# A weight's low part written by ScalarE and finished by a GpSimd DMA instead of VectorE: one layer in split float32

## The chip, the cores and the metric

The kernel runs on one core of one Trainium2 chip. The metric is the device time of one execution in microseconds (us), shown as a median of several. Each profile below is of one execution, with the time of every instruction on the engines: PE is TensorE, DVE is VectorE, ACT is ScalarE, POOL is GpSimd, SP is SyncE, which here issues loads and stores.

## The reference: one encoder layer

One layer on 512 tokens of 1024 features, all in float32:

```
x = LN1(alpha*x + 0.5*SwiGLU1(x))                 # weights 1024x2816, 1024x2816, 2816x1024
h = x @ w_in                                      # q, k, v, indexer q/k/w, conv B, C, u
A = attention over the 128 keys that an indexer picks for each query (ALiBi, softmax)
B = bg * causal_conv3(cg * u)
x = LN2(alpha*x + concat(A, B) @ w_out)
x = LN3(alpha*x + 0.5*SwiGLU2(x))
x = x + sigmoid(x @ ple_gate_w) * (p @ ple_proj_w)
```

## The kernel before: every operand in two parts

**Two parts.** TensorE multiplies in a rounded format (float32r). So every operand is kept as a high part, `hi = round(w)`, and a low part, `lo = w - hi`, and a product is the sum of three matmuls: hi with hi, and twice a high part with a low part. The second of the three to four matmuls on a block already needs a low part, so a weight of which only the high part is there lets PE go on for one or two matmuls at most. `split` (line 110) makes the parts: ACT casts (line 111), DVE subtracts (line 112).

**Weights.** `unit` (line 114) brings in a piece of a weight of 128 x 1024 values (512 KB): a load issued by SP (line 118) into a raw page, then `split` into a high and a low page, then the raw page is free again. There are 98 such pieces in the program: all of the down projections (44), `w_in` (29, one of them narrower), `w_out` (8), `ple_gate_w` (8), `ple_proj_w` (2) and `p` (1), and the gate and up weights of three plain chunks (6): the second chunk of the first SwiGLU and the first two of the second. The gate and up weights of the other chunks go through `weights` (line 270), which forms sums of quarter blocks (seven products instead of eight) and splits these with `split` itself.

**Pages.** All weights, hidden chunks and projections live in 38 pages of 4 KB per partition, handed out first in, first out. A load waits until the last reader of its page is done, and SP issues its loads in order.

**Order.** A scheduler orders each engine's instructions by priorities; `unit` raises the priority of its load and its split by a number (`AHEAD...`) so that they run ahead of their use. On the chip each engine runs its own list strictly in order and waits at its head. POOL's list has few entries: index tables (lines 536 and 537) and, for each of the three layer norms, four tiny powers (line 160), whose results DVE needs for the last step of the norm (line 162), after which PE transposes the block (line 146).

**Places that the prediction names.** The start: two plain chunks of the first SwiGLU. The end of the first SwiGLU, where the last down-projection pieces come in (PE line 132). The end of the attention, where `w_out` is multiplied. The end of the second SwiGLU, and behind it the gate (`ple_gate_w`), whose eight pieces are read in order, three matmuls each.

Of the kernel before, what the change touches and what calls it, by code (L numbers as in the profile page):

```python
# [10 lines left out]
ALU = mybir.AluOpType  # L11
# [52 lines left out]
def layer_kernel(ctx: ExitStack, tc: tile.TileContext, x, ln1_g, ln1_b, ffn1_wg, ffn1_wu, ffn1_wd, w_in,  # L64
                 conv_w, w_out, ln2_g, ln2_b, ffn2_wg, ffn2_wu, ffn2_wd, ln3_g, ln3_b, ple_gate_w, ple_proj_w, x_t, p_t, out):
    nc = tc.nc
# [19 lines left out]
    def page(shape, dt=F32R):  # L86
        i = free_pages.pop(0)
        t = sb.tile(shape, dt, tag=f"pg{i}", name=f"pg{i}_{count('pg')}")
        owner[id(t)] = (i, t)
        return t  # L90

    def free(*tiles):
        for t in tiles:
            free_pages.append(owner.pop(id(t))[0])
# [15 lines left out]
    def split(hi, lo, src):  # L110
        nc.scalar.copy(hi, src)  # L111
        nc.vector.tensor_sub(lo, src, hi.bitcast(F32))  # L112

    def unit(src, shape, ahead=AHEAD):

        with tc.high_priority(offset=ahead):
            r = page(shape, F32)
            nc.sync.dma_start(r, src)
            hi, lo = page(shape), page(shape)
            split(hi, lo, r)  # L120
            free(r)
        return hi, lo

# [115 lines left out]
    def ffn(X, wg, wu, wd, ln_g, ln_b, first, load_nat, groups, nplain, ahead, ahead_f, ahead_d):  # L239
# [11 lines left out]
        def plain(fc, ws, cuts, ah):  # L251

            for nm, w in mats:
                if nm not in ws:
                    ws[nm] = unit(rows(w[:, fc * P:(fc + 1) * P], 0, NDC), [P, NDC, P], ah)
            ps = {nm: bank("all") for nm, _ in mats}
            for n in range(2):
                for nm, _ in mats:
                    mm(ps[nm][:, n * 256:(n + 1) * 256],
                       [((ws[nm][0][:, c], ws[nm][1][:, c]), tuple(z[:, c % 4] for z in X.q[f"B{c // 4 + 1}{n + 1}"])) for c in range(NDC)])  # L260
            for u in ws.values():
                free(*u)
            hf = ring("hf", 2, [P, 512])
            s_t = ring("a", 2, [P, 512])
            nc.scalar.activation(s_t, ps["g"], AF.Silu)
            nc.vector.tensor_mul(hf, s_t, ps["u"])
            return put(hf)
# [80 lines left out]
        for gi, per in enumerate(groups):  # L348
# [13 lines left out]
            def wd_rows(i, half):  # L362
                if (i, half) not in wds:
                    n2 = min(2, per - i)
                    u = unit(rows(wd[:, half * 512:(half + 1) * 512], (f0 + i) * P, n2), [P, n2, 512], ahead_d)
                    for k in range(n2):
                        wds[i + k, half] = (u[0][:, k], u[1][:, k])
                        held[i + k, half] = u if k == n2 - 1 else ()
                return wds[i, half]
# [38 lines left out]
    def embed_prep():  # L408
        p_T.extend(unit(rows(p_t, 0, 2), [P, 2, S], AHEAD_P))
        yield  # L410
        for k in range(2):
            wp.append(unit(rows(ple_proj_w[0], k * P, 1), [P, 1, 1024], AHEAD_P))
# [384 lines left out]
```

## Time and profile before

| | before |
|---|---|
| time, median of 3 | 1025.05 us (1024.97 to 1025.1) |
| the profiled execution's own time | 1026.09 us |
| its span, first to last instruction | 1024.0 us |
| PE busy | 1004.6 us (98%) |
| DVE busy | 822.2 us (80%) |
| ACT busy | 441.8 us (43%) |
| DMA from HBM | 101.49 MB |

The share of busy time is an average over stages. Times in a view count from the span's start; about 2 us of the execution lie outside the span. Where a group's row says `<-`, the name behind it is what ended the idle time, by its engine, its output and its line.

### The profile page before, as it was taken

The page shows a single profiled execution, that of the slowest core. Times are in us where ns is not written, and L with a number is a line of the kernel's source. Part 1 is how long each engine was busy: PE and PEld are TensorE (multiplying, and loading weights), DVE is VectorE, ACT ScalarE, POOL GpSimd, SP SyncE. Part 2 cuts the span into 40 slices and gives each one's busy share as a digit, 9 for nine tenths or more (in the row PEclk, how much of TensorE's full clock was granted, in tenths as well). Part 3 has the DMA queues.
Part 4 walks back from the last instruction along what each step waited for, and adds up shares of the span by engine and source line. Part 5 has one row for each costly group of instructions (what it writes and reads, how often), then busy time and mean ns, then how long its engine had stood idle before and what let it go on. Part 6 is the DMA issues. An engine that isn't in the chain of part 4 may idle for free.

```text
span 1024.0 us, 15507 instructions
## 1 busy us (share of the span) xinstructions
PE 1004.6 (98%) x6313; PEld 903.8 (88%) x6313; DVE 822.2 (80%) x1283; ACT 441.8 (43%) x621; POOL 25.0 (2%) x35
## 2 busy tenths in 40 slices
PE   8999999999999999999999999999999999999998
PEld 7989999898998878888878778989999898998787
DVE  7897868978697958999479988896868969689852
ACT  6444424433354235332576836443425324246221
POOL 1000000000000200000000011000000000000100
PEclk9999999999999999999999999999999999999999
DMA  9342324323335231424013223331424322227111
GB/s 311 122 123 83 109 98 131 97 83 107 100 119 185 69 92 42 128 58 124 20 42 104 83 65 101 124 124 39 127 83 144 103 79 87 83 85 265 52 41 51
DMA packets 99510, 104.57 MB, mean 102 GB/s; under 512 B 5872, under 2 KB 81904, under 8 KB 99440
## 3 DMA queue, kind: packets, MB, share of 16 engines
q1 hardware_dynamic: 99440, 103.60, 31.8%
q8 instruction: 49, 0.80, 0.3%
q14 instruction: 21, 0.17, 0.1%
HBM read 101.49 MB, written 2.10 MB: 101 GB/s over the span
## 4 chain that ended last, share of the span: by engine, by line
PE 89%; DMA 4%; DVE 3%; ACT 3%; issue 1%; POOLq 0%; SPq 0%; ACTq 0%
PE bk L132 86%; ACT pg L111 2%; DVE pg L112 1%; DMA pg<-in_ffn_wu_dram 1%; PE bk L506 1%; DMA pg<-in_w_in_dram 1%; DMA pg<-in_x_t_dram 1%; PE bk L507 1%; PE bk L704 1%; DMA pg<-in_ple_proj_w_dram 1%; DMA pg<-in_ffn_wd_dram 0%; PE bk L146 0%; ACT a L676 0%; DMA pg<-in_ple_gate_w_dram 0%; PE bk L692 0%
## 5 line engine op out<-in xcount | busy, mean ns | idle before, releaser
L132 PE MATMUL bk<-pg,pg 128*128 128x256 f32 (+1 forms) x2832 | 496.4, 333 | 4.4 <-ACT pg L111 1.8
L132 PEld LDWEIGHTS bk<-pg,pg 128*128 128x128 f32 x2832 | 427.6, 190 | 56.0 <-ACT pg L111 2.6
L111 ACT CAST pg<-pg 128x1024 fp32r<-128x1024 f32 (+1 forms) x267 | 260.0, 984 | 313.3 <-PE bk L132 78.4
L112 DVE TENSOR_TENSOR pg<-pg,pg 128x1024 fp32r<-128x1024 f32 (+1 forms) x267 | 300.6, 1139 | 40.6 <-ACT pg L111 35.5
L132 PE MATMUL bk<-xq,pg 128*128 128x256 f32 x2208 | 275.3, 284 | 4.6 <-DVE mv L158 1.5
L132 PEld LDWEIGHTS bk<-xq,pg 128*128 128x128 f32 x2208 | 270.6, 193 | 7.0 <-ACT pg L111 2.3
L132 PE MATMUL bk<-xT,pg 128*128 128x512 f32 (+2 forms) x600 | 133.0, 381 | 0.3 <-ACT xT L111 0.2
L132 PEld LDWEIGHTS bk<-xT,pg 128*128 128x128 f32 (+1 forms) x600 | 109.9, 186 | 21.5 <-ACT xT L111 0.5
L132 PE MATMUL bk<-pg,xT 128*128 128x512 f32 (+1 forms) x312 | 69.5, 374 | 1.3 <-DVE nat L385 1.3
L132 PEld LDWEIGHTS bk<-pg,xT 128*128 128x128 f32 x312 | 55.0, 188 | 11.4 <-ACT pg L111 1.8
L329 ACT ACTIVATE a<-pg 128x512 f32<-128x512 f32 x40 | 25.2, 629 | 71.7 <-DVE pg L338 66.1
L111 ACT CAST pg<-hf 128x512 fp32r<-128x512 f32 (+1 forms) x56 | 34.6, 618 | 35.2 <-DVE hf L330 19.6
L112 DVE TENSOR_TENSOR pg<-hf,pg 128x512 fp32r<-128x512 f32 (+1 forms) x56 | 38.3, 684 | 4.7 <-ACT pg L111 4.5
L399 DVE SCALAR_TENSOR_TENSOR nat<-bk,nat 128x512 f32<-128x512 f32 x64 | 40.4, 682 | 0.8 <-PE bk L132 0.7
L330 DVE TENSOR_TENSOR hf<-a,pg 128x512 f32<-128x512 f32 x40 | 27.5, 688 | 13.6 <-ACT a L329 13.5
L338 DVE TENSOR_TENSOR pg<-bk,pg 128x512 f32<-128x512 f32 x20 | 13.8, 692 | 29.9 <-PE bk L132 29.4
L160 POOL TENSOR_TENSOR mv<-mv,mhalf 128x1 f32<-128x1 f32 x12 | 17.8, 1480 | 627.0 <-DVE mv L159 627.0
L286 DVE TENSOR_TENSOR pg<-pg,pg 128x512 f32<-128x512 f32 x40 | 27.3, 686 | 5.7 <-DMA pg<-in_ffn_wg_dram 5.7
L292 DVE TENSOR_TENSOR pg<-pg 128x512 f32<-128x512 f32 x40 | 27.4, 686 | 2.9 <-PE bk L132 2.9
L112 DVE TENSOR_TENSOR pg<-bk,pg 128x512 fp32r<-128x512 f32 (+2 forms) x37 | 22.5, 626 | 8.5 <-ACT pg L111 8.1
L287 DVE TENSOR_TENSOR pg<-pg,pg 128x512 f32<-128x512 f32 x40 | 27.3, 685 | 0.0
L293 DVE TENSOR_TENSOR pg<-pg,pg 128x512 f32<-128x512 f32 x40 | 27.1, 686 | 0.1
(100 smaller groups left out, 612.7 us busy)
## 6 DMA issues: line engine op xcount, KB each, us to landing
pg<-in_ffn_wg_dram SPq DMA_DIRECT2D x44, 512.0 KB, 4.1
pg<-in_ffn_wu_dram SPq DMA_DIRECT2D x44, 512.0 KB, 4.7
pg<-in_ffn_wd_dram SPq DMA_DIRECT2D x44, 512.0 KB, 4.0
pg<-in_w_in_dram SPq DMA_DIRECT2D x28, 512.0 KB, 3.6
pg<-in_w_out_dram SPq DMA_DIRECT2D x8, 512.0 KB, 3.9
pg<-in_ple_gate_w_dram SPq DMA_DIRECT2D x8, 512.0 KB, 4.8
pg<-in_x_t_dram SPq DMA_DIRECT2D x4, 512.0 KB, 7.5
nat<-in_x_dram SPq DMA_DIRECT2D x4, 512.0 KB, 8.9
```

The source lines that it names most:

```text
L111: nc.scalar.copy(hi, src)
L112: nc.vector.tensor_sub(lo, src, hi.bitcast(F32))
L132: nc.tensor.matmul(ps, lhsT=st[a], rhs=mv[b], start=first and i == 0 and k == 0, stop=last and i == n - 1 and k == 2)
L160: nc.gpsimd.tensor_tensor(mv[:, 3:4], mv[:, 2:3], mhalf, op=ALU.pow)
L286: nc.vector.tensor_add(S1, A21, A22)
L287: nc.vector.tensor_sub(S2, S1, A11)
L292: nc.vector.tensor_sub(S3, A11, A21)
L293: nc.vector.tensor_sub(S4, A12, S2)
L329: nc.scalar.activation(s_t, e[m][:, :, 0], AF.Silu)
L330: nc.vector.tensor_mul(h3, s_t, e[m][:, :, 1])
L338: nc.vector.tensor_add(e[0][:, 1], prod("S4", "B22"), u4)
L399: nc.vector.scalar_tensor_tensor(dst, acc[t], CY, dst, op0=ALU.mult, op1=ALU.add)
```

## The change

In `unit` alone DVE's subtraction is gone. ACT writes the high part as before, and then a second time reads the raw page and writes its negative, rounded the same way, into the low page. Then a DMA issued by GpSimd adds the raw page to the low page where it lies: `-hi + w`. The raw page is free when this DMA has landed. `split` stays as it is everywhere else.

```diff
             r = page(shape, F32)
             nc.sync.dma_start(r, src)
             hi, lo = page(shape), page(shape)
-            split(hi, lo, r)
+            nc.scalar.copy(hi, r)
+
+            nc.scalar.mul(lo, r, -1.0)
+            nc.gpsimd.dma_start(lo, r, accum_op=ALU.add)
             free(r)
         return hi, lo
```

Lines behind this one move by three: a line 132 of before is a line 135 of the changed kernel, and a piece's own lines are 120 (cast), 122 (negative) and 123 (DMA).

The scheduler orders the engines anew. In the lists below `pg_n` is the n-th page handed out, the last number a running number. **POOL at the end of the program** held only the powers of the last norms:

```order
L160 TENSOR_TENSOR mv_5942<-mv_5942,mhalf 128x1
L160 TENSOR_TENSOR mv_5999<-mv_5999,mhalf 128x1
L160 TENSOR_TENSOR mv_9451<-mv_9451,mhalf 128x1
L160 TENSOR_TENSOR mv_9513<-mv_9513,mhalf 128x1
L160 TENSOR_TENSOR mv_9575<-mv_9575,mhalf 128x1
L160 TENSOR_TENSOR mv_9637<-mv_9637,mhalf 128x1
```

Now the DMAs of the gate's pieces stand among the last norm's four powers:

```order
L123 DMA pg_949_9771<-pg_947_9768 128x1024
L163 TENSOR_TENSOR mv_9541<-mv_9541,mhalf 128x1
L163 TENSOR_TENSOR mv_9603<-mv_9603,mhalf 128x1
L123 DMA pg_952_9778<-pg_950_9775 128x1024
L163 TENSOR_TENSOR mv_9665<-mv_9665,mhalf 128x1
L123 DMA pg_955_9785<-pg_953_9782 128x1024
L123 DMA pg_958_9792<-pg_956_9789 128x1024
L163 TENSOR_TENSOR mv_9727<-mv_9727,mhalf 128x1
L123 DMA pg_961_9799<-pg_959_9796 128x1024
```

The DMA of the gate's last piece (page 961) stands behind the last norm's fourth power.

**PE in the gate's first bank.** `ident,nat` are the transposes of the last norm's last block; the pieces' pages are 939 to 961 by threes, the first of a pair the high part. Before, 24 matmuls of the first bank and five of the second stood ahead of the transposes:

```order
L132 MATMUL bk_9705<-pg_957_9695,xT_3_9371 128x512
L132 MATMUL bk_9705<-pg_958_9696,xT_3_9371 128x512
L132 MATMUL bk_9705<-pg_957_9695,xT_3_9372 128x512
L132 MATMUL bk_9705<-pg_960_9701,xT_3_9371 128x512
L132 MATMUL bk_9705<-pg_961_9702,xT_3_9371 128x512
L132 MATMUL bk_9705<-pg_960_9701,xT_3_9372 128x512
L132 MATMUL bk_9736<-pg_939_9659,xT_3_9371 128x512
L132 MATMUL bk_9736<-pg_940_9660,xT_3_9371 128x512
L132 MATMUL bk_9736<-pg_939_9659,xT_3_9372 128x512
L132 MATMUL bk_9736<-pg_942_9665,xT_3_9371 128x512
L132 MATMUL bk_9736<-pg_943_9666,xT_3_9371 128x512
L146 MATMUL bk_9643<-ident,nat_71 128x128 x4
```

Now 20 of the first bank stand ahead of them, and four more behind them before the low page 961 is read:

```order
L135 MATMUL bk_9803<-pg_957_9791,xT_3_9455 128x512
L135 MATMUL bk_9803<-pg_958_9792,xT_3_9455 128x512
L149 MATMUL bk_9733<-ident,nat_71 128x128 x4
L149 MATMUL bk_9740<-ident,nat_71 128x128 x4
L135 MATMUL bk_9803<-pg_957_9791,xT_3_9456 128x512
L135 MATMUL bk_9803<-pg_960_9798,xT_3_9455 128x512
L135 MATMUL bk_9834<-pg_939_9749,xT_3_9455 128x512
L135 MATMUL bk_9834<-pg_940_9750,xT_3_9455 128x512
L135 MATMUL bk_9803<-pg_961_9799,xT_3_9455 128x512
```

So the transposes have come forward by nine matmuls.

**ACT at the end of the second SwiGLU** (920 to 950 us in the profile). Page 929 is the raw page of a down-projection piece, 930 its high and 931 its low page; line 329 is the activation of the last chunk. Before:

```order
L111 CAST pg_942_9665<-pg_941_9663 128x1024
L111 CAST pg_930_9415<-pg_929_9413 128x1024
L111 CAST pg_936_9439<-pg_935_9437 128x1024
L329 ACTIVATE a_9361<-pg_913_9167 128x512
L111 CAST pg_924_9388<-pg_923_9386 128x1024
L111 CAST pg_917_9364<-hf_9360 128x512
```

Now:

```order
L120 CAST pg_930_9502<-pg_929_9500 128x1024
L332 ACTIVATE a_9445<-pg_913_9251 128x512
L122 ACTIVATE pg_931_9503<-pg_929_9500 128x1024
L111 CAST pg_917_9448<-hf_9444 128x512
L120 CAST pg_924_9473<-pg_923_9471 128x1024
L122 ACTIVATE pg_925_9474<-pg_923_9471 128x1024
```

The negative of page 929 stands behind the last chunk's activation, and the cast of page 923 behind the one of the hidden chunk (917).

## Rows read from the trace of the kernel before

**Rows 1.** The page: engine, busy us, share of the span, instructions.

```profile
PE 1004.6 (98%) x6313; PEld 903.8 (88%) x6313; DVE 822.2 (80%) x1283; ACT 441.8 (43%) x621; POOL 25.0 (2%) x35
```

**Rows 2.** The page's chain that ended last, shares of the span.

```profile
PE 89%; DMA 4%; DVE 3%; ACT 3%; issue 1%; POOLq 0%; SPq 0%; ACTq 0%
```

**Rows 3.** Waits of PE: who waited for whom, us in total, times, longest.

```profile
PE bk L132 <- DVE nat L739: 1.6, 2, 0.8
...
PE bk L132 <- DVE mv L158: 1.5, 1, 1.5
...
PE bk L132 <- DVE nat L385: 1.3, 1, 1.3
PE bk L506 <- DVE ss L675: 1.3, 2, 0.6
```

**Rows 4.** Groups by line and shape on ACT, DVE, POOL: busy us, mean ns, idle before.

```profile
L111 ACT CAST pg<-pg 128x1024 fp32r<-128x1024 f32 x226 | 235.8, 1050 | 270.3 <-PE bk L132 63.4 <-DVE pg L287 56.4 <-DMA pg<-in_ffn_wd_dram 47.3
...
L112 DVE TENSOR_TENSOR pg<-pg,pg 128x1024 fp32r<-128x1024 f32 x226 | 273.5, 1221 | 37.7 <-ACT pg L111 33.0 <-ACT a L329 2.7 <-PE bk L132 1.7
...
L160 POOL TENSOR_TENSOR mv<-mv,mhalf 128x1 f32<-128x1 f32 x12 | 17.8, 1480 | 627.0 <-DVE mv L159 627.0
L537 POOL TENSOR_SCALAR a<-dm 128x512 f32<-128x512 f32 x1 | 1.8, 1784 | 0.0
```

**Rows 5.** Line 118, the 98 loads of the pieces: issue to landing.

```profile
DMA to landing us min/median/max: 3.0/3.9/8.9
```

**Rows 6.** Windows, 0 to 30 us: us, busy (instructions) by engine, clock, DMA share, GB/s.

```profile
0.00:30.00 30.00, 25.46 (x164) 22.34 (x165) 22.47 (x24) 17.93 (x19) 2.83 (x19) 0.94 0.92 280
```

**Rows 7.** Timeline, the start: start us, us, engine, line, operation, count, [idle before].

```profile
15.40 1.04 ACT L111 CAST pg<-pg 128x1024 fp32r<-128x1024 f32 x1
...
17.08 1.05 ACT L111 CAST pg<-pg 128x1024 fp32r<-128x1024 f32 x1 [0.64 <-DMA pg<-in_ffn_wg_dram]
...
21.15 6.04 PE L132 MATMUL bk<-xq,pg 128*128 128x256 f32 x49
```

**Rows 8.** Timeline, the last down-projection piece of the first SwiGLU.

```profile
328.33 1.03 ACT L111 CAST pg<-pg 128x1024 fp32r<-128x1024 f32 x1
328.47 0.69 DVE L330 TENSOR_TENSOR hf<-a,pg 128x512 f32<-128x512 f32 x1 [0.82 <-ACT a L329]
...
331.37 0.76 PEld L132 LDWEIGHTS bk<-pg,pg 128*128 128x128 f32 x4 [0.42 <-DVE pg L112]
```

**Rows 9.** Timeline, the end of the attention, where `w_out` begins.

```profile
583.13 0.62 ACT L111 CAST pg<-hf 64x512 fp32r<-64x512 f32 x1
...
586.80 2.34 PE L132 MATMUL bk<-pg,pg 128*128 128x512 f32 x9 [0.82 <-DVE pg L112]
```

**Rows 10.** Timeline, the end of the second SwiGLU.

```profile
939.21 0.62 ACT L329 ACTIVATE a<-pg 128x512 f32<-128x512 f32 x1
...
941.69 14.14 PE L132 MATMUL bk<-pg,pg 128*128 128x512 f32 x61 [0.74 <-ACT pg L111]
```

**Rows 11.** Timeline, the gate and the last norm's fourth power.

```profile
974.50 6.74 PE L132 MATMUL bk<-pg,xT 128*128 128x512 f32 x29
...
975.55 1.23 DVE L112 TENSOR_TENSOR pg<-pg,pg 128x1024 fp32r<-128x1024 f32 x1 [0.20 <-ACT pg L111]
...
978.68 1.45 POOL L160 TENSOR_TENSOR mv<-mv,mhalf 128x1 f32<-128x1 f32 x1 [9.30 <-DVE mv L159]
...
981.60 1.07 PE L146 MATMUL bk<-ident,nat 128*128 128x128 f32 x8 [0.37 <-DVE nat L162]
```

**Rows 12.** Timeline, a down-projection piece in the middle of the second SwiGLU.

```profile
721.19 1.05 ACT L111 CAST pg<-pg 128x1024 fp32r<-128x1024 f32 x1 [4.03 <-DMA pg<-in_ffn_wd_dram]
...
724.88 7.31 PE L132 MATMUL bk<-pg,pg 128*128 128x256 f32 x54
```

**Rows 13.** Windows, 540 to 600 us, columns as in rows 6.

```profile
540.00:600.00 60.00, 57.33 (x307) 47.17 (x306) 53.39 (x139) 40.37 (x89) 0.00 (x0) 1.00 0.30 97
```

## The prediction

> **What bounds the kernel now.** I read the page first: PE is busy in 98% of the span, DVE in 80%, ACT in 43% [rows 1]. The chain that ended last runs 89% through PE, 3% through DVE and 3% through ACT [rows 2]. So PE's own work is the bound, and work taken off DVE can return only what PE waits for DVE. The list of PE's waits has four such entries apart from the pieces themselves, 1.6 + 1.5 + 1.3 + 1.3 = 5.7 us in all [rows 3]; that is the most that relief of DVE can give there. The other way round, every microsecond that a weight's low part comes later than PE reaches it is a microsecond of span. So the question is at which places a piece arrives just in time, and how much later it will now be.
>
> **What a piece costs, now and then.** DVE loses 98 subtractions of 1.22 us, about 120 us of work [rows 4]. ACT gets 98 more passes; the nearest row is its cast of the same shape, 1.05 us [rows 4], so about 103 us, which its idle 57% takes in. Before, a low part was ready 1.22 us after the cast, if DVE was free. Now it is ready after ACT's second pass, 1.05 us, and then X, the time from the end of that pass until the DMA has landed.
>
> No row shows a DMA issued by GpSimd, so X is bounded by the loads of the same 98 pieces: they land 3.0 us after their issue at the least, 3.9 in the median, 8.9 at the most [rows 5]. In the first 30 us the DMA engines are busy at 0.92 and move 280 GB/s, so full use is 304 GB/s and one piece, 0.524 MB, takes 1.7 us of it [rows 6]. Of the median load 3.9 - 1.7 = 2.2 us are then fixed. The accumulation has to read two pages, the raw one and the low one, where a load reads one: 2 x 1.7 = 3.4. To this I add 0.9 for GpSimd's issue, taken between nothing and the 1.48 us that its smallest steady instruction takes [rows 4]. **X = 2.2 + 3.4 + 0.9 = 6.5 us.** The ends are 3.0 (as the fastest load, issue and second read free) and 8.9 + 1.7 = 10.6 (as the slowest load, with a second read).
>
> A rule of the Trainium skill speaks for less: the page "DMA: Bandwidth & Descriptors", section on the anatomy of a DMA from GpSimd, gives 2.0 us and the bytes at 436 GB/s, as an estimate 3.2 us for a piece. No run here shows it yet; by it the sum below would come out near the low end. Against it stands "Collectives: The Full Stack", section on the bandwidth ceiling: an add in the DMA engines is slower because it reads two sources.
>
> **Where it is just in time.** Five places, each by the same step: when is the low part ready, and when does PE reach it.
>
> *Start.* ACT casts one piece from 15.40 and the next from 17.08 [rows 7]; with the second passes between, the second piece's negative ends at 19.4, ready at 25.9. PE's row from 21.15 runs at 0.12 us a matmul and meets that low page first as its 15th, 22.9 [rows 7]; the new order pulls nine others ahead of it, 24.0. **1.9 us.** Ends: 0 and 6.0.
>
> *End of the first SwiGLU.* The last down-projection piece is cast until 329.36, and PE started on its low part at 331.37 [rows 8]. The negative ends at 330.4. In POOL's new order two index operations stand ahead of this DMA, the second of 1.78 us [rows 4], behind DVE's step that ended at 329.2 [rows 8] and that the new ACT order lets come earlier; the issue falls between 330.4 and 332.3, taken at 331.4. Ready at 337.9: **6.5 us**; ends 2.0 and 11.5.
>
> *Where `w_out` begins.* PE already waited here for a subtraction, until 586.80 [rows 9]. The negative of that piece now stands behind the last head's cast, which ended at 583.75 [rows 9], and up to one exponential: it ends at about 585.4 and is ready at 591.9: **5.1 us**; ends 1.0 (584.8 without the exponential) and 9.2.
>
> *End of the second SwiGLU.* The negative of page 929 follows the activation that ended at 939.83: 940.9, ready at 947.4. PE goes on at 941.69 with 0.23 us a matmul and reaches it after two high parts, 942.2 [rows 10]: **5.2 us**; ends 1.7 and 9.3. The piece behind it is ready 0.6 + 1.05 + 1.05 = 2.7 us later (two casts and a negative), and PE comes to it after eleven matmuls, 2.5.
>
> *The gate.* The last piece's DMA stands behind the fourth power on POOL, which ended at 980.13 [rows 11]. One of the pieces' subtractions, 1.23 us behind 0.20 of idle time, stood just ahead of that norm's last steps on DVE [rows 11]; it is gone, so I put them 1.4 us earlier: 978.7, and ready at 985.2. PE runs 20 matmuls from 974.50 at 0.23, transposes at 980.2 instead of 981.60, runs four more until 982.2 and waits 3.0. It then still has five matmuls (1.2) to do that before stood ahead of the transposes, which ended at 982.67 [rows 11]: 985.2 + 1.2 - 982.7 = **3.7 us**; ends 0.7 and 7.8.
>
> **Where it is free, and what covers it.** In the middle of a SwiGLU a piece has time before its use. A tight one there: cast until 722.24, then a hidden chunk's cast of 0.6, then the negative until 723.9, ready at 723.9 + 6.5 = 730.4; PE comes to it after 48 matmuls of its row from 724.88, at 730.7 [rows 12]. The cover is 0.3 us; above X = 6.8 each of three such groups starts to pay. The raw page is free 1.05 + 6.5 - 1.22 = 6.3 us later, and SP's queue waits in order for pages; the loads behind it there are as early as this one, so I take nothing and leave the risk to the upper side. The powers on POOL come behind DMAs only where their own norm's PE work is as late.
>
> **Sum.** 1.9 + 6.5 + 5.1 + 5.2 + 3.7 = 22.4 us of new waits. Of the 5.7 us that PE waited for DVE [rows 3] I take back half, 2.8, since after a freed DVE ACT or PE itself is next: 22.4 - 2.8 = 19.6. The profiled execution took 1026.09 us, 1.04 above the median of 1025.05; the sum goes on the median: **1044.6 us**. With the low ends (0 + 2.0 + 1.0 + 1.7 + 0.7 = 5.4) and half relief it is 1027.6; with the high ends (43.8) and 10.6 - 6.8 = 3.8 more in three groups it is 55.2 - 2.8 = 52.4 more, 1077.
>
> **The rivals.**
> *The add is hidden and DVE's relief is left (the other side).* If X is near 3.0, the waits are 5.4 us and full relief is 5.7: 1024.8, no change. It ends faster by over 2 us from X below about 2.4: at 2.0 the waits are 0 + 1.0 + 0 + 0.7 + 0.7 = 2.4 and the time 1021.8. For it speaks the fastest load [rows 5]; against it the second read and that the relief must be whole. I take 1025. Chance 0.13. The rule on the fixed cost named above would make it this one: with 3.2 us, 1025 to 1028.
> *The adds queue.* X goes to 10 and more because several land at once beside loads (the start's DMA share is 0.92 [rows 6]), and the middle of the SwiGLU pays too: 1077. Against it: elsewhere the DMA engines have room (0.30 [rows 13]). Chance 0.2.
> *ACT becomes the one that is waited for.* Between 540 and 600 us ACT is busy for 40.4 of 60 us [rows 13], and six more passes of 1.05 fall there among the exponentials that the last heads wait for. If all lie on the path, 6.3 us beside the sum: 1051. Against it: a third of that window is idle on ACT. Chance 0.12.
> *As forecast*, X between about 4.5 and 8.5: 0.55, for itself 1036 to 1054.
>
> **The numbers.** A measurement of this kernel tells changes of over 0.2%, 2 us, from none. Only the first rival can end within or below that: 0.06 faster, 0.05 the same; the rest 0.89 slower. The range leaves out the lower half of the first rival and the upper part of the second: 1027 to 1072.
>
> **What would show it.** The profile after should have POOL DMAs at line 123 landing about 6 us after their issue; PE waits on these DMAs at the five places, near 24, 331, 587, 942 and 982 us plus what came before, of 2 to 7 us each and 22 in all; no PE wait in the middle of the SwiGLU stages; DVE busy near 703 us and ACT near 545. The prediction is wrong if landing takes 3 or 10 us, if the relief of DVE is the larger part, or if PE's new waits are at places where I found cover: then a queue (SP's pages, POOL's order) delayed something that I took as early.

## The result, and the profile after

| | before | changed |
|---|---|---|
| time, median of 3 | 1025.05 us | 1088.85 us (1087.39 to 1093.01) |
| the profiled execution's own time, its span | 1026.09, 1024.0 us | 1088.85, 1087.0 us |
| PE busy, idle in the span | 1004.6, 19.4 us | 1027.0, 60.0 us |

The ratio is 1.0631, 95% interval 1.0586 to 1.0677: 64 us slower, where 20 were forecast. The direction was right and the size was not; the time lies above the range.

The page of the changed kernel, busy time and then the chain that ended last (against [rows 1, 2]):

```profile
PE 1027.0 (94%) x6313; PEld 920.5 (85%) x6313; DVE 717.0 (66%) x1185; ACT 528.2 (49%) x719; POOL 107.0 (10%) x133
...
PE 80%; DMA 9%; issue 6%; ACT 2%; POOL 1%; DVE 1%; SPq 0%; POOLq 0%; ACTq 0%
```

DVE gave up 105 us and ACT took 86 more, and neither decides: the chain lost 9 points on PE and gained 5 on DMA and 5 on "issue" (time in which an engine waited for nothing that the profile shows). PE has the same 6313 instructions, yet its busy time grew by 22.4 us, and its idle time by 40.6. These two make the 63 us of the span. Who PE waits for (against [rows 3]):

```profile
PE bk L135 <- DMA pg<-pg: 33.7, 10, 5.6
PE bk L149 <- DVE nat L165: 5.4, 4, 4.6
PE bk L135 <- ACT pg L427: 3.4, 1, 3.4
PE bk L707 <- ACT pg L111: 2.9, 1, 2.9
PE bk L509 <- DVE ss L678: 2.0, 1, 2.0
```

`DMA pg<-pg` is GpSimd's add. Ten waits for adds, 33.7 us, are most of the new idle time. PE runs the same number of instructions in both traces, so the start of its n-th instruction can be subtracted, place by place (near the changed places the n-th instruction is not always the same piece of work, since the order changed a little):

| place (PE's n-th instruction) | forecast | later by | of it idle | of it in slower matmuls |
|---|---|---|---|---|
| start (0 to 200) | 1.9 | 10.2 | 6.5 | 3.8 |
| middle of the first SwiGLU (to 1920) | 0 | 0.0 | 0.0 | 0.0 |
| its end (to 2310) | 6.5 | 10.4 | 7.6 | 2.8 |
| first norm, `w_in` begins (to 2640) | 0 | 8.0 | 6.3 | 1.7 |
| indexer, conv, q and k (to 3160) | 0 | 0.0 | 0.0 | 0.0 |
| last heads, `w_out`, second norm (to 3740) | 5.1 | 10.9 | 5.4 | 5.5 |
| middle of the second SwiGLU (to 5600) | 0 | 0.5 | 0.0 | 0.5 |
| its end (to 6090) | 5.2 | 17.1 | 11.7 | 5.4 |
| gate (to 6200) | 3.7 | 5.8 | 3.0 | 2.8 |
| sum | 22.4 | 63.0 | 40.5 | 22.4 |

(The sums are of unrounded values.) So the five places that were named all pay, each 1.6 to 5.4 times what was forecast; the first norm, 8.0 us, was not named. PE's timeline at the start, at the end of the first SwiGLU, at the end of the second, and in the gate (against [rows 7, 8, 10, 11]):

```profile
27.55 1.65 PE L135 MATMUL bk<-xq,pg 128*128 128x256 f32 x6 [5.24 <-DMA pg<-pg]
31.34 7.43 PE L135 MATMUL bk<-xq,pg 128*128 128x256 f32 x38 [2.13 <-DMA pg<-pg]
...
340.93 1.94 PE L135 MATMUL bk<-pg,pg 128*128 128x512 f32 x4 [4.49 <-DMA pg<-pg]
346.99 15.04 PE L135 MATMUL bk<-pg,pg 128*128 128x512 f32 x56 [4.12 <-DMA pg<-pg]
...
975.79 1.71 PE L135 MATMUL bk<-pg,pg 128*128 128x256 f32 x12
981.70 5.80 PE L135 MATMUL bk<-pg,pg 128*128 128x512 f32 x15 [4.19 <-DMA pg<-pg]
993.14 12.95 PE L135 MATMUL bk<-pg,pg 128*128 128x512 f32 x49 [5.64 <-DMA pg<-pg]
1009.23 3.06 PE L135 MATMUL bk<-pg,pg 128*128 128x512 f32 x8 [3.14 <-DMA pg<-pg]
...
1038.03 1.65 PE L135 MATMUL bk<-pg,xT 128*128 128x512 f32 x3 [2.61 <-DMA pg<-pg]
1040.49 0.80 PE L135 MATMUL bk<-pg,xT 128*128 128x512 f32 x1 [0.81 <-DMA pg<-pg]
```

Two things are to be read there. One place has two or three waits and not one: the next pieces are late too. And behind a wait a matmul takes longer: 15 in 5.80 us are 0.39 us each, three in 1.65 are 0.55, where 61 took 14.14 before, 0.23 each [rows 10]. Windows of the changed kernel around the second SwiGLU's end (columns as in [rows 6]):

```profile
972.00:976.00 4.00, 4.00 (x35) 4.00 (x35) 1.87 (x4) 4.00 (x6) 0.86 (x1) 1.00 0.76 237
980.00:986.00 6.00, 4.30 (x10) 3.44 (x11) 1.36 (x2) 3.41 (x4) 0.87 (x1) 0.50 1.02 295
997.00:1009.00 12.00, 9.09 (x41) 7.17 (x39) 2.77 (x4) 2.00 (x2) 1.99 (x3) 1.00 0.98 214
970.00:1000.00 30.00, 20.16 (x100) 17.03 (x99) 5.90 (x9) 19.54 (x22) 6.94 (x8) 0.77 1.00 256
```

Ahead of the wait PE was granted 1.00 (2.4 GHz); from 980 to 986, in and behind the wait of 4.19 us, 0.50 (1.2 GHz). That is where the 22.4 us of longer busy time come from: over the whole span PE was busy for 48.6 us at 0.50, and before for 3.4 us; half of the difference is 22.6. And from 970 to 1000 us the DMA engines are full, share 1.00. In the same place before it was 0.43, with as many loads issued there:

```profile
930.00:960.00 30.00, 29.26 (x161) 24.94 (x160) 27.57 (x37) 14.61 (x17) 2.64 (x2) 1.00 0.43 156
```

What filled them stands in the page's queues (packets, MB, share of 16 engines), and GpSimd's side in its groups and its DMAs' time from issue to landing:

```profile
q1 hardware_dynamic: 99440, 103.60, 30.0%
q0 software_dynamic: 14112, 51.16, 25.4%
...
L123 POOL DMA_DIRECT2D pg<-pg x98 | 85.8, 876 | 889.2 <-ACT pg L122 548.5
...
DMA to landing us min/median/max: 4.5/5.5/11.7
```

An add holds all 16 DMA engines for 0.254 x 1087.0 / 98 = 2.82 us. A load of the same 0.524 MB holds them for 0.300 x 1087.0 / (103.60 / 0.524) = 1.65 us, in the mean of all loads. The Trainium skill, "Collectives: The Full Stack", section on the bandwidth ceiling, says that an add in the DMA engines is slower because it reads two sources. The 1.7 times a load that were measured fit that; the reads themselves are not in the trace. The Trainium skill, "DMA: Bandwidth & Descriptors", section on the anatomy of a DMA from GpSimd, gives an estimate of 3.2 us for a piece. Here the fastest add landed 4.5 us after its issue and the median 5.5, and the measurement decides.

The loads beside the adds land later as well. Two rows of the DMA issues (count, size, median us from issue to landing), before and then changed:

```profile
pg<-in_ffn_wd_dram SPq DMA_DIRECT2D x44, 512.0 KB, 4.0
pg<-in_ple_gate_w_dram SPq DMA_DIRECT2D x8, 512.0 KB, 4.8
...
pg<-in_ffn_wd_dram SPq DMA_DIRECT2D x44, 512.0 KB, 5.3
pg<-in_ple_gate_w_dram SPq DMA_DIRECT2D x8, 512.0 KB, 7.9
```

### The profile page after: what moved, and what is told of

The parts are those of the page before. It is cut to its first block, busy times and chain, and to the rows that moved or that the text cites. A ratio compares the mean times of both kernels' runs of the same rounds, so it can differ in the third digit from the quotient of the medians.

```text
span 1087.0 us, 15826 instructions
## 1 busy us (share of the span) xinstructions
PE 1027.0 (94%) x6313; PEld 920.5 (85%) x6313; DVE 717.0 (66%) x1185; ACT 528.2 (49%) x719; POOL 107.0 (10%) x133
## 3 DMA queue, kind: packets, MB, share of 16 engines
q1 hardware_dynamic: 99440, 103.60, 30.0%
## 4 chain that ended last, share of the span: by engine, by line
PE 80%; DMA 9%; issue 6%; ACT 2%; POOL 1%; DVE 1%; SPq 0%; POOLq 0%; ACTq 0%
PE bk L135 77%; DMA pg<-pg 3%; DMA pg<-in_w_in_dram 3%; DMA pg<-in_ffn_wu_dram 1%; DMA pg<-in_x_t_dram 1%; PE bk L509 1%; POOL pg L123 1%; DMA pg<-in_ffn_wd_dram 1%; PE bk L510 1%; ACT pg L122 1%; PE bk L707 1%; PE bk L149 0%; DMA pg<-in_p_t_dram 0%; PE bk L695 0%; ACT pg L120 0%
## 5 line engine op out<-in xcount | busy, mean ns | idle before, releaser
L135 PE MATMUL bk<-pg,pg 128*128 128x256 f32 (+1 forms) x2832 | 509.1, 338 | 26.7 <-DMA pg<-pg 22.9
L135 PEld LDWEIGHTS bk<-pg,pg 128*128 128x128 f32 x2832 | 435.6, 193 | 81.8 <-DMA pg<-pg 25.5
L112 DVE TENSOR_TENSOR pg<-pg,pg 128x1024 fp32r<-128x1024 f32 (+1 forms) x169 | 181.9, 1092 | 14.0 <-ACT pg L111 10.8
L123 POOL DMA_DIRECT2D pg<-pg x98 | 85.8, 876 | 889.2 <-ACT pg L122 548.5
L122 ACT ACTIVATE pg<-pg 128x1024 fp32r<-128x1024 f32 (+1 forms) x98 | 102.6, 1051 | 24.6 <-PE bk L135 10.7
L135 PE MATMUL bk<-pg,xT 128*128 128x512 f32 (+1 forms) x312 | 71.8, 381 | 4.3 <-DMA pg<-pg 3.4
L402 DVE SCALAR_TENSOR_TENSOR nat<-bk,nat 128x512 f32<-128x512 f32 x64 | 39.9, 680 | 0.0
L388 DVE SCALAR_TENSOR_TENSOR nat<-bk,nat 128x512 f32<-128x512 f32 x16 | 11.0, 687 | 41.3 <-PE bk L135 41.3
L289 DVE TENSOR_TENSOR pg<-pg,pg 128x512 f32<-128x512 f32 x40 | 27.2, 683 | 6.3 <-DMA pg<-in_ffn_wg_dram 6.3
```

The lines of the kernel that those rows point to most:

```text
L122: nc.scalar.mul(lo, r, -1.0)
L123: nc.gpsimd.dma_start(lo, r, accum_op=ALU.add)
L135: nc.tensor.matmul(ps, lhsT=st[a], rhs=mv[b], start=first and i == 0 and k == 0, stop=last and i == n - 1 and k == 2)
L289: nc.vector.tensor_add(S1, A21, A22)
L402: nc.vector.scalar_tensor_tensor(dst, acc[t], CY, dst, op0=ALU.mult, op1=ALU.add)
```

## The experiments

Times are compared with runs of the kernel before on the same chip, whose median there was 1027.0 to 1027.5 us; "over before" is the difference of medians. The change itself costs 64 us (1088.85 against 1025.05). In the cuts of code, "..." stands for lines left out. Theories: **latency** (the forecast: PE waits X for each low part, nothing else changes), **traffic** (the adds fill the DMA engines where pieces come in bursts, so loads and adds queue), **pages** (the raw page is released 6 us later), **order** (GpSimd's in-order queue and its limits), **ACT** (its second pass).

**Is it the DMA at all?** DVE adds in place of it.

```diff
-            nc.gpsimd.dma_start(lo, r, accum_op=ALU.add)
+            nc.vector.tensor_add(lo, lo.bitcast(F32), r)
```

> All 98 pieces as in the changed kernel, but VectorE adds the raw page to the low page where GpSimd's DMA did. If the loss lies in the DMA (its latency, its traffic or GpSimd's queue), nearly all of the 64 us goes: only ScalarE's second pass, 1.05 us, is left in front of a just-in-time piece, five places, so 1025 + 5 = 1030 us (1024 to 1037). If ScalarE's 103 us of second passes are the cause, more than half of the loss stays: over 1057.

1039.18 us, ratio 1.0123 (1.0108 to 1.0139): 12 over before, somewhat more than expected. So ACT's second pass, with DVE's add behind it, is a small part; the difference, some 50 us, belongs to the DMA.

**Pieces with cover.** Only the 32 down-projection pieces outside the last groups are changed (a flag of `unit` chooses; the others go through `split`).

```diff
...
+            if far:
+                nc.scalar.copy(hi, r)
+                nc.scalar.mul(lo, r, -1.0)
+                nc.gpsimd.dma_start(lo, r, accum_op=ALU.add)
+            else:
+                split(hi, lo, r)
...
```

> The change only for the 32 down-projection pieces that are not in a SwiGLU's last group; all others are split by VectorE as before. The forecast's own step (these pieces have cover) says no change: 1025 us, within 2. If adds in the middle hold back later loads or pages, it is 1030 or more. If VectorE's relief were worth something by itself, it would be below 1023.

1031.93 us, ratio 1.004 (1.0025 to 1.0055): a miss by a little. The cover holds but for 5 us, and DVE's relief buys nothing here.

**GpSimd's limit of DMAs in flight.** The changed kernel with more room for descriptors (a warm-up tile shares another one's place to make it).

```diff
-    warm = sb.tile([P, 512], F32, name="warm")
+    warm = sb.tile([P, 512], F32, tag="hf0", name="warm")
...
-    nc = _bacc.Bacc("TRN2", target_bir_lowering=False, num_devices=1, dynamic_dma_scratch_size=1024)
+    nc = _bacc.Bacc("TRN2", target_bir_lowering=False, num_devices=1, dynamic_dma_scratch_size=3584)
```

> The changed kernel with 3584 instead of 1024 bytes per partition of space for GpSimd's DMA descriptors (and the warm-up tile laid over another one to make room). In the trace of the changed kernel a fourth DMA was never issued before an earlier one had landed. If that limit costs time, the waits of GpSimd named issue (15.9 us) go and the time falls by 5 us or more, to below 1084. If the 16 DMA engines are the limit there (their share is 1.00 from 328 to 350 and from 970 to 1000 us), more adds in flight only land later each: 1086 to 1092.

1089.26 us: unchanged. GpSimd's waits for "issue" went from 15.9 us to 0.5, and the slowest add lands 13.3 us after its issue in place of 11.7. More adds in flight gained nothing, as it must be if the engines are what they wait for.

**Traffic without a wait for it.** DVE splits; then an add that nothing reads.

```diff
             split(hi, lo, r)
+            nc.gpsimd.dma_start(r, r, accum_op=ALU.add)
             free(r)
```

> The low part made by VectorE as before; behind it a DMA of GpSimd adds the raw page to itself, and nothing reads it: the traffic, GpSimd's queue and the later release of the raw page stay, the wait of TensorE on an add goes, and ScalarE has no second pass. By the forecast's theory (a low part that comes X later) nothing is left: 1025 to 1030 us. If the adds' traffic delays the loads behind them where loads come in bursts, a good part of the loss stays: 1045 to 1065. If only GpSimd's order matters (powers behind DMAs): 1030 to 1035, lost in the layer norms.

1092.67 us, ratio 1.0644 (1.0603 to 1.0685): 65 over before, though PE waits for no add. The latency theory falls as the whole story. That the sum equals the change's is in part chance: in its profiled execution (1100.71 us, the slowest of four) 19.3 us are lost in the middle of the first SwiGLU, where the change loses nothing, and at the start none. At the other places it loses nearly what the change does (table below). Its list of PE's waits:

```profile
PE bk L133 <- ACT pg L111: 28.7, 9, 10.3
PE bk L147 <- DVE nat L163: 12.5, 4, 5.1
```

PE waits for ACT's casts now, and these for their loads (ACT's waits for loads from `w_in` and the down projection alone are 124 us, and before 82.5): the adds push the loads back. At the start, with DVE's split, PE's 200th instruction was 1.7 us earlier than before; so the start's 10.2 us come with the wait for the add itself.

**Queue and page without traffic.** The same place, but the DMA moves 16 rows of 256 bytes.

```diff
+            z = r[0:16, 0, 0:64]
+            nc.gpsimd.dma_start(z, z, accum_op=ALU.add)
```

> VectorE splits as before; behind it a tiny DMA of GpSimd (16 rows of 256 bytes of the raw page, added to themselves, read by nobody). It keeps 98 DMAs in GpSimd's queue and holds the raw page for some 3 us longer, but moves next to nothing. Traffic theory (the adds fill the DMA engines): 1027, below 1032 us. Page theory (raw pages come free later, so loads start later): about half of the loss, since the hold is about half: 1045 to 1065. Order theory (powers and other work of GpSimd behind DMAs): 1030 to 1040, lost in the layer norms.

1030.08 us, ratio 1.0023 (1.0009 to 1.0037). Such a DMA landed 1.9 us after its issue (row of the DMA issues):

```profile
pg<-pg POOLq DMA_DIRECT2D x98, 4.0 KB, 1.9
```

So 98 DMAs in GpSimd's queue and pages held for some 2.5 us longer cost 3 us.

**The same, held longer.** Three tiny DMAs in a row, each waiting for the one ahead.

```diff
...
+            for _ in range(3):
+                nc.gpsimd.dma_start(z, z, accum_op=ALU.add)
```

> VectorE splits as before; behind it three tiny DMAs of GpSimd, each waiting for the one ahead, on the raw page (16 rows of 256 bytes). One of them landed 1.9 us after its issue, so the page is held for about 6 us, as long as by the changed kernel's add, with next to no traffic. Page theory: 1065 or more. Traffic theory: 1030 to 1045, most of it at the layer norms, whose powers now stand behind DMAs that wait.

1055.97 us, 29 over before: between what the theories gave. Most of PE's waits are for the norms, whose powers stand behind DMAs that wait. At the first SwiGLU's end PE was 0.2 us early, and at the second end the longest wait for a piece was 0.4 us, so held pages cost next to nothing at either end:

```profile
PE bk L149 <- DVE nat L165: 16.3, 6, 6.2
```

**Scarce pages, and traffic without a hold.** The kernel before with 36 pages, and then with a full add from the low page into tiles of its own (`junk`, two of them), the raw page freed at once.

```diff
-NPAGES = 38
+NPAGES = 36
...
             split(hi, lo, r)
...
+            nc.gpsimd.dma_start(z, lo.bitcast(F32), accum_op=ALU.add)
             free(r)
```

> The kernel before with 36 instead of 38 pages: what scarcer pages cost without any DMA of GpSimd, and the control of the next kernel. Page theory: pages are tight everywhere, 1040 us or more. Traffic theory: up to 1035.

> 36 pages; VectorE splits as before and the raw page is freed at once, as before; a DMA of GpSimd of full size adds the low page to a tile of its own, read by nobody. Full traffic, no hold of the raw page. Traffic theory: 40 to 65 us above the kernel with 36 pages and no DMAs. Page theory: within 10 us of it.

1040.27 and 1078.93 us: 36 pages cost 13 us, and the traffic 39 on top, just under the 40 to 65 of its theory. Part of the 39 is GpSimd waiting 90 us for its two tiles in turn, with the norms' powers behind, so this run alone doesn't settle it.

**Pages, directly.** For 67 pieces the DMA adds the weights from HBM again, and the raw page is free before it.

```diff
-            nc.gpsimd.dma_start(lo, r, accum_op=ALU.add)
+            nc.gpsimd.dma_start(lo, src if shape[-1] >= 512 else r, accum_op=ALU.add)
```

> The changed kernel, but for 67 of the 98 pieces (those with rows of 2 KB or more) the DMA of GpSimd adds the weights from HBM a second time and not from the raw page, so that the raw page is free after ScalarE's second pass, as early as before. The same number of adds and bytes, the same wait for the low part. Page theory (raw pages released 6 us late delay the loads): more than half of the 64 us goes, below 1055. Traffic theory: little changes, 1075 to 1095.

1168.81 us, which neither theory gave. GpSimd's timeline shows a limit: the second of two adds was issued only when the first had landed, 8 us later:

```profile
784.48 1.22 POOL L123 DMA_DIRECT2D pg<-in_ffn_wd_dram  x1 [51.68 <-DVE pg L340]
792.45 1.21 POOL L123 DMA_DIRECT2D pg<-in_ffn_wd_dram  x1 [6.75 <-ACT pg L120]
```

With the room for descriptors of the third experiment:

> The kernel whose adds take 67 pieces from HBM, with 3584 instead of 1024 bytes for GpSimd's DMA descriptors. In its first run the second of two adds was issued only when the first had landed (792.45 after 792.13 us), so it measured that limit and not the pages. With the limit away: page theory below 1055 us, traffic theory 1075 to 1095.

1085.14 us, ratio 1.0556 (1.0521 to 1.059). The 84 us that came back belong to the room for descriptors. With the pages of 67 pieces free early, 58 of the 64 us are still there: the page theory falls as a main cause. (An add held the engines a little longer here, 0.268 x 1084.4 / 98 = 2.97 us.)

**GpSimd computes the add itself.**

```diff
-            nc.gpsimd.dma_start(lo, r, accum_op=ALU.add)
+            nc.gpsimd.tensor_tensor(lo, lo.bitcast(F32), r, op=ALU.add)
```

> The changed kernel, but GpSimd adds the raw page to the low page itself, with one instruction of its own in place of the DMA: the low part comes some 2 to 4 us after ScalarE's second pass, the raw page is held as long, GpSimd's order is the same, and there is no traffic. Traffic theory: 1035 to 1050 (somewhat over the kernel in which VectorE adds, 1039). Page or order theory: 1060 to 1090.

1075.87 us, 49 over before without any DMA traffic: a miss. PE's two longest sums of waits:

```profile
PE bk L149 <- DVE nat L165: 10.8, 6, 3.0
PE bk L135 <- POOL pg L123: 10.3, 6, 4.4
```

GpSimd does one add after the other, 2.5 us each, with the norms' powers in the same list, and DVE's subtractions take longer beside it (last section). How the 49 us divide among these was not tested. So this run speaks neither for the traffic nor against it.

**The powers of the norms.** The changed kernel without them (a constant of 1 stands in their place, so the norms are not scaled).

```diff
...
-        nc.gpsimd.tensor_tensor(mv[:, 3:4], mv[:, 2:3], mhalf, op=ALU.pow)
...
```

> The changed kernel without the twelve powers of the layer norms on GpSimd (a constant of 1 takes their place, so the norms are not scaled). If DMAs ahead of the powers in GpSimd's queue are a main cause, over 10 us go, most of it at the first norm where TensorE waited 4.6 us: below 1079. If the bursts are, the norms' waits only turn into waits for the same late pieces: 1080 to 1090.

1089.88 us: nothing gained. That a power stood behind a DMA at the first norm is no cause of the loss.

**Are the places independent?** The change for the two pieces of the start, for the 20 of the two ends (last groups and gate), and for the other 76, each by the flag alone.

> The change only for the two pieces at the start. In the changed kernel TensorE's matmul 200 came 10.2 us later than before, 6.5 of it idle and 3.8 in matmuls at the lower clock, and with VectorE's split and the same traffic it came 1.7 us earlier. If a low part that is late there costs what stands there, 1025 + 10 = 1035 us. If the start is caught up later, 1027.

> The change only for the 20 pieces at the two ends: the last group's down projections of both SwiGLUs (12) and the gate (8). There the pieces come in bursts. Traffic theory: the burst alone makes the loss, about 10 us at the first end and 20 at the second: 1050 to 1060 us. If what is lost there came from the pieces ahead (pages held, queues filled in the middle), less than half of it: below 1040.

> The change for the 76 pieces that are neither at the start nor at the two ends. If the places are independent, what the other two kernels did not show is here: 63 - 10 (start) - 28 (ends) = 25 us, so 1052 (1045 to 1060). If the ends and the start are what matters and the rest only moves their loss, below 1040.

1037.00, 1054.83 and 1047.63 us: 10.0 + 27.8 + 20.4 = 58 of 64 us over before. All three came as expected, and the ends need nothing from ahead of them. The missing six lie within the intervals (the change's own is 60 to 69 us). Place by place the sum is less exact: at the first SwiGLU's end the 20 and the 76 pieces lose 7.7 and 5.7 us alone and 10.4 together, at the first norm 0.6 and 2.8 alone and 8.0 together.

**Dose at the ends.** Every second of the 20 pieces.

```diff
...
+        far = far and count("far") % 2 == 0
...
```

> As the kernel with the 20 end pieces changed (1054.8 us, 28 over before), but only every second of them: 10 adds. Traffic theory, counted by the burst: the eleven pieces at the second end take 11 x 1.65 of loads + 5.5 x 2.82 of adds = 34 us of the full DMA engines in place of 49, where 23 were used before; the loss there should fall to less than half, and the whole to 1034 to 1042. If each late low part costs the same by its own latency, half of 28 is left or, as waits overlap, more: 1041 to 1055.

1047.24 us, 20 over before in place of 28: a miss of the traffic count in sum, and inside what separate latencies gave. By place, in the profiled executions, it divides: at the second SwiGLU's end PE was 10.1 us late in place of 21.0; at the first end 5.0 in place of 7.7, and in the gate 5.8 in place of 6.0. In the gate halving the number saved nothing. (The profiled execution with 20 pieces took 1060.40 us, 5.6 above its median, so the 21.0 may be high, and that the second end fell to half is not certain.)

**Traffic at the ends without the wait.** As the fourth experiment, for the 20 pieces alone.

```diff
...
+                split(hi, lo, r)
+                nc.gpsimd.dma_start(r, r, accum_op=ALU.add)
...
```

> The same 20 end pieces, but VectorE splits them, and behind the split GpSimd's DMA adds the raw page to itself, which nothing reads: the traffic of the ends without a wait for an add, and without ScalarE's second pass. Traffic theory: two thirds or more of the 28 us stay, 1045 or more. Latency theory (each late low part costs its own delay): less than a third, below 1036.

1058.37 us, 31 over before where the 20 pieces cost 28: all of it without a wait for an add and without ACT's second pass. PE's waits:

```profile
PE bk L136 <- ACT pg L111: 13.4, 6, 6.5
PE bk L150 <- DVE nat L166: 7.1, 2, 4.2
PE bk L136 <- DVE pg L112: 5.1, 5, 2.0
```

The gate's loads landed 7.7 us after their issue in the median, and before 4.8. The two powers ahead of the norm waits (L166) each started when DVE had its input, not behind an add. Place by place, us later than before in the profiled executions (their times stand in the head of the table):

| place | change, 1088.85 | 20 end pieces, 1060.40 | traffic at the ends alone, 1055.60 | traffic of all pieces, 1100.71 |
|---|---|---|---|---|
| start | 10.2 | -0.9 | -0.9 | -1.7 |
| middle of the first SwiGLU | 0.0 | 0.0 | 0.0 | 19.3 |
| its end | 10.4 | 7.7 | 8.6 | 14.9 |
| first norm | 8.0 | 0.6 | 0.1 | 6.9 |
| last heads, `w_out`, second norm | 10.9 | 0.2 | -0.2 | 12.2 |
| middle of the second SwiGLU | 0.5 | 0.0 | 0.0 | 1.0 |
| its end | 17.1 | 21.0 | 16.3 | 16.2 |
| gate | 5.8 | 6.0 | 5.7 | 5.3 |

So at both ends and in the gate the adds make the loss without being waited for, and held pages alone did not (three tiny DMAs). At the first norm and around `w_out` the traffic of all pieces loses about as much as the change, but it was not tried there by itself. At the start it loses nothing.

**The clock.** The kernel with the 20 end pieces, with idle matmuls at the second end.

```diff
...
+                                for _ in range({(0, 0): 26, (0, 4): 10, (1, 0): 12}.get((half, i), 0)):
+                                    nc.tensor.matmul(dummy, lhsT=h[0][:, 0, :P], rhs=h[0][:, 0], start=True, stop=True)
...
```

> The kernel with the 20 end pieces changed (1054.8 us), with 48 idle matmuls in three blocks (26, 10, 12) where TensorE waited for low parts at the second SwiGLU's end, into a bank that nobody reads. At full rate they take 48 x 0.23 = 11 us, and TensorE waited 6.3 + 5.3 + 3.0 us there; 8.8 us more went into slower matmuls. If the lower clock follows TensorE's waiting, the fill takes the place of waits and the clock stays up: 5 to 8 us less, 1047 to 1050. If the clock falls there anyway, the time is the same or, where a block comes at the wrong place, up to 11 us more: 1054 to 1066.

1065.67 us, 38 over before where the kernel without the fill is 28 over: a miss in time. Windows without the fill, then with it:

```profile
940.00:947.00 7.00, 5.03 (x41) 4.71 (x40) 3.18 (x5) 7.00 (x9) 1.77 (x2) 1.00 0.89 260
948.00:954.50 6.50, 3.19 (x8) 2.51 (x9) 1.39 (x2) 1.75 (x3) 0.97 (x2) 0.50 1.01 277
```

```profile
940.00:955.00 15.00, 12.23 (x74) 10.62 (x72) 4.64 (x7) 10.50 (x14) 3.50 (x4) 1.00 0.91 260
957.00:969.00 12.00, 4.18 (x10) 3.15 (x10) 0.00 (x0) 7.78 (x8) 2.85 (x4) 0.50 0.93 193
```

Where 26 idle matmuls stood in place of the wait of 6.28 us, the clock stayed at 1.00 until 955, where it had been 0.50 from 948. But the work that they stood ahead of, and the pieces behind it, came later too, PE waited 2.84 and then 7.82 us at the next pieces, and the clock fell there. That the lower clock follows PE's waits is shown; that filling them gains time is not.

## Why the prediction was wrong

**What failed.** One term that was used wrongly, and one that is missing. The first is "X = 2.2 + 3.4 + 0.9 = 6.5 us", used as a delay that every piece has by itself, also where pieces come in bursts. Measured from the end of ACT's second pass to the landing, by stretch (median):

| stretch, us | pieces | X |
|---|---|---|
| start | 2 | 9.8, 11.6 |
| 40 to 310 | 16 | 5.7 |
| 310 to 370 (end of the first SwiGLU) | 12 | 8.8 |
| 370 to 575 | 27 | 5.5 |
| 575 to 640 (`w_out`) | 8 | 5.1 |
| 640 to 955 | 19 | 6.1 |
| 955 to 1045 (second end, gate) | 14 | 9.7 |

Over all pieces the median is 6.0, so the size for one add was sound. But a place is just in time because many pieces come at once there, and there an add is a load on a shared resource: 1.65 us of the DMA engines became 1.65 + 2.82. At the second end before, eleven loads were issued from 920.0 and had landed by 947.3; now eleven loads and the ten adds among them need 11 x 1.65 + 10 x 2.82 = 46 us of full engines, and from the first load's issue at 960.0 to the last of these adds' landing it was 51.7, with a DMA share of 0.90. At the first end eleven pieces need 11 x 4.47 = 49 us, and took 52.8, with a share of 0.94. The time of a burst, not the time of one DMA, was the term to work out, and its numbers were there: 304 GB/s of full use stood in the prediction.

The second is the load behind an add. The prediction asks for it only in the middle of a SwiGLU and only through the page that is held ("the loads behind it there are as early as this one, so I take nothing and leave the risk to the upper side"). There it was right, 0.0 and 0.5 us. Where pieces come in bursts its sum has no such term. But the loads share the engines with the adds: the two runs with adds that nothing reads lose 65 and 31 us without one wait for an add. Late loads and late adds are not two terms that add up: the engines serve both, and PE waits for whichever comes last.

The trace of the changed kernel shows the order of causes at the second end. The first nine of the eleven loads were issued 40 us later than before, which is what had been lost by then, so no page held them back; but the eighth and the ninth landed 10.6 and 12.8 us after their issue, and before 6.0 and 5.2. Only the tenth and eleventh were issued 12 us late on top, each right behind the landing of an add (990.62, 996.10 us), which frees a page. And a late load holds up what stands behind it in ACT's list: PE's wait until 1009.23 was for a down-projection piece whose second pass ended only at 996.45, though all six of these loads had landed by 983.03; in between ACT worked on pieces of the gate and waited 1.8 and 1.9 us for their loads.

**What was left out.** 22.4 of the 63 us are slower matmuls behind waits, at a granted clock of 0.50. No term of the sum had it.

**Point by point.** DVE's busy time was put near 703 and came to 717, ACT's near 545 and came to 528. No PE wait in the middle of the SwiGLU stages: right, 0.5 us. PE's waits for adds at the five places: right in place (27 to 31, 341 to 347, 626, 982 to 1009, 1038 to 1040 us), 33.7 in place of 22. DVE's relief was taken as 2.8 us: of the four waits of [rows 3], 5.7 us, L388's 0.9 and L678's 2.0 are left, so it came to the 2.8 that were taken, and the norms' waits for L165 (5.4 and 1.5, where 0.9 stood before) took it back. (Two more of PE's waits for DVE before, 0.9 us each, were left out of the 5.7.) The start, 1.9 forecast, is the largest miss by ratio: X was 9.8 and 11.6 beside the loads, and the lower clock stands on top.

**The rivals.** "The adds queue" (1077 us, chance 0.2) names what happened at the bursts, without the clock; the middle of the SwiGLU, which it let pay too, did not. "ACT becomes the one that is waited for" happened in part: around `w_out`, X was only 5, but PE waited 3.4 + 2.9 us for ACT (list above), and the place cost 10.9 where 5.1 were forecast. The add was hidden at none of the five places.

**What stays open.** The 8.0 us at the first norm were not divided into late loads of `w_in` and ACT's order; the powers did not make them, and neither end pieces nor the others made them alone. The 10.9 us around `w_out` were not divided into traffic and ACT's second passes. No version that was tried beats the kernel before.

## What to carry to other kernels

Work that is moved onto the DMA engines is to be priced twice: as a latency where one piece is just in time, and as engine time where pieces come in bursts, and there every load behind it is late as well. Look for the places where the consumer waits next to nothing now; they are where loads bunch, so an average landing time doesn't hold there. A wait of TensorE costs more than its length: here 41 us of waits brought 22 us of slower matmuls. Taking work off an engine that next to nothing waited for returned nothing here.

## What the runs showed of the hardware

GpSimd's add of a piece took 2534 ns, and DVE's own subtractions took longer beside it. Groups of DVE in the changed kernel, then with GpSimd adding:

```profile
L112 DVE TENSOR_TENSOR pg<-pg,pg 128x1024 fp32r<-128x1024 f32 x129 | 155.8, 1219 | 9.5 <-ACT pg L111 6.5 <-ACT a L332 2.7
L112 DVE TENSOR_TENSOR pg<-hf,pg 128x512 fp32r<-128x512 f32 x48 | 32.9, 686 | 29.4 <-ACT pg L111 29.4
...
L112 DVE TENSOR_TENSOR pg<-bk,pg 128x512 fp32r<-128x512 f32 x20 | 13.3, 683 | 1.7 <-ACT pg L111 1.5
```

```profile
L123 POOL TENSOR_TENSOR pg<-pg,pg 128x1024 fp32r<-128x1024 f32 x97 | 244.9, 2534 | 725.7 <-ACT pg L122 719.7 <-DVE pg L557 2.5 <-POOL pg L123 2.0
...
L112 DVE TENSOR_TENSOR pg<-pg,pg 128x1024 fp32r<-128x1024 f32 x129 | 165.5, 1293 | 11.0 <-ACT pg L111 5.9 <-PE bk L135 3.2 <-issue 1.7
L112 DVE TENSOR_TENSOR pg<-hf,pg 128x512 fp32r<-128x512 f32 x48 | 47.2, 984 | 17.0 <-ACT pg L111 16.8
...
L112 DVE TENSOR_TENSOR pg<-bk,pg 128x512 fp32r<-128x512 f32 x20 | 13.2, 682 | 3.3 <-ACT pg L111 3.2
```

With both inputs in SBUF the mean rose from 686 to 984 ns; with one in PSUM (`bk`) it stayed at 683. The mean mixes two kinds: of the 48 (`hf`), the ten that overlapped an add of GpSimd in time took 2121 ns in the mean and the other 38 took 684, so DVE was not slowed throughout but held in a few of them. Of the 20 with an input in PSUM six overlapped one, and took 680 ns. DVE's busy time was 797 in place of 717 us for the same instructions. The Trainium skill, "SBUF — State Buffer", section on the two separate sides, says that DVE and GpSimd share a port pair, and that a two-input DVE operation meets GpSimd there only when both inputs are in SBUF; these rows agree.

With 1024 bytes for descriptors GpSimd had three adds between pages in flight and never a fourth; with 3584 bytes a fourth was issued five times.
